# A two-block transformer kernel: 16 latent-attention heads between the steps of a projection, full 128-column tiles, bias rows loaded from a shifted table, negated differential scores

## The chip, the cores and the metric

The program runs on one core of one Trainium2 chip and is launched once. The metric is the device time of an execution in microseconds. The kernel before was timed three times: 2095.17, 2100.26 and 2096.01 us, the median is 2096.01 us.

## The reference

The input is 512 tokens of width 1024, everything in fp32. Two transformer blocks run one after the other. The change concerns only the attention of the first; the second block (sparse attention, a gated delta rule, a mixture of 32 experts) and the first block's FFN are the same in both kernels.

The first block computes `z = rms_norm(x) @ w_in` and splits it into latents for one attention (MLA) and queries, keys and values for another (differential):

```python
# MLA: 8 heads, width 96 (64 + 32 with rope), values 64 wide
q = (rms_norm(q_lat) @ w_uq);  kv = (rms_norm(kv_lat) @ w_ukv)
k = concat([k_nope, broadcast(k_rope)]);  q, k = rms_norm(q), rms_norm(k)   # then rope
logits = where(allowed, q @ k.T * 96 ** -0.5, -1e30)
y_mla = softmax(logits) @ v
# differential: 4 heads, two queries and two keys of width 64 each (m = 0, 1), values 128 wide
logits[m] = where(allowed, rms_norm(dq[m]) @ rms_norm(dk[m]).T * 64 ** -0.5 + bias, -1e30)
probs = softmax(logits)
y_diff = rms_norm((probs[0] - lam * probs[1]) @ dv) * (1 - lam_init)
# both
x = x + concat([y_mla, y_diff]) @ w_out
```

`allowed` lets a query see the keys of its own chunk of 64 tokens and of all chunks before it. `bias` is a table of 32 rows per head, looked up by a bucket of (key position - query position).

## The kernel before

The first block's attention is `block1_attention`. Tokens lie in four blocks of 128; the three projections of `w_in` behind the latents (`grp` 1: differential keys, 2: differential values, 0: differential queries) are sums over 8 slices of 128 channels, each with three matmuls, since every fp32 operand is split into a high and a low part in TensorE's fast fp32 form (L469 to L471). In plain fp32, which scores, transposes and value products use, the trace shows two instructions for each matmul of the program and one for each transpose.

- *Bias* (L416 to L440). A matmul makes the row `fv` of 640 values for each head, one for each difference of positions. The row goes to a buffer `fd` in DRAM, on ScalarE's queue. Four loads (L436) read it with overlapping rows, row p starting at element p; that is the bias mirrored along the queries, so a matmul with a flipped identity (`flip`, L438) turns it over and VectorE copies it out (L439) and masks a corner (L440).
- *MLA heads' inputs.* The generator `heads()` (as `bg`) makes queries, keys and values of the MLA heads; its steps stand between the matmuls of `grp` 1 and 2.
- *Queries' projection.* `grp` 0 is computed last, slice by slice for all four token blocks, then written out, squared and summed; `turn()` normalises and transposes each block, and its steps are spread over the attention (`next(turns, None)`).
- *Steps of the attention.* `mla_step(i, hp)` handles two MLA heads of query block i, with keys 0 to 128(i+1): scores (L526, PSUM pool `acc`), maximum (L528, VectorE), exponential and its sum (L531, ScalarE), reciprocal (L533) and scaling of the probabilities (L534, VectorE); in a second part transposes (L541) and their copy to SBUF (L543); in a third the value product (L552), with V as the stationary operand: two 64-column tiles side by side in the array, so that the output comes out transposed. `diff_step(i, h)` does the same for one differential head with two score tiles: four matmuls of 64 rows by 64 columns (L566), two each at the same time in different quarters of the array, then bias and maximum in one VectorE operation, a negation (L575), exponentials, two reciprocals, and their combination; transposes at L590, value product at L598.
- *Order.* It is written out by hand: `steps` holds 12 MLA steps (blocks 0 to 2), 16 differential steps, 4 MLA steps (block 3). Each round starts a step's first part, then runs the next part of the steps still open (`pend`). The attention's first step follows the queries' projection.
- *Queues and pools.* SP's queue carries the weights, ScalarE's and GpSimd's the small tensors. `self.adp`, the pool of the second block's `w_ada` tiles (loaded by GpSimd's queue at L862), is allocated ahead of the attention, on the other side of SBUF.

## Time and profile before

| | before |
|---|---|
| median of 3 runs | 2096.01 us |
| profiled execution, own time | 2101.31 us |
| its span, first to last instruction | 2099.5 us |
| mean granted TensorE clock | 0.979 |
| TensorE busy | 1995.3 us (95%) |
| VectorE busy | 1206.0 us (57%) |
| ScalarE busy | 734.9 us (35%) |
| GpSimd busy | 218.0 us (10%) |

The profile comes from one execution. Its times count from the first instruction. PE is TensorE, PEld its loading of stationary operands (beside the matmuls), DVE VectorE, ACT ScalarE, POOL GpSimd. A matmul counts as busy from its start to its modelled end, so matmuls overlap in the records and the step from one start to the next says more than a duration. "L552" is a line of the kernel; "O<-PT,V" are the tiles written and read. In brackets stands the idle time ahead of an instruction and what ended it. In the 2099.5 us, the attention that the change touches ends near 242 us.

### The profile page before, as it was taken

Reading aid. Unit: us, or ns where it says so; the run is one execution under the profiler, and the core shown is the slowest. Engines: PE = TensorE matmul, PEld = TensorE weight load, DVE = VectorE, ACT = ScalarE, POOL = GpSimd, SP = SyncE. Lnnn points to the kernel's source line nnn. Section 1 sums busy time; section 2 is a strip of 40 time slices with the busy share of each in tenths; the row PEclk is TensorE's granted clock in tenths of the full one; section 3 lists DMA queues with packets and bytes.
Section 4 is the critical chain, followed back from the end, with each engine's and each line's share of the span. In section 5 each row is a group of like instructions: output and inputs, shape, how many; then the busy total and the mean of one; then the engine's idle time right before and its main releaser. Section 6 shows DMA issues by size and latency. Waiting matters only on the chain.

```text
span 2099.5 us, 33715 instructions
## 1 busy us (share of the span) xinstructions
PE 1995.3 (95%) x12921; PEld 1395.7 (66%) x12921; DVE 1206.0 (57%) x2577; ACT 734.9 (35%) x1405; POOL 218.0 (10%) x227
## 2 busy tenths in 40 slices
PE   8999999999999998998989989999988999999995
PEld 6764788788888777676777878788854444444441
DVE  5867678666666757898384674554465223223234
ACT  4456533232233434335253544542222122122121
POOL 0000001000100013013131131010003000000000
PEclk9998999999999999999999999999989999999998
DMA  7210237554532432122111211263677999999991
GB/s 235 61 41 11 77 123 221 161 170 144 184 101 91 146 112 71 41 86 71 47 51 42 96 36 47 96 221 117 239 294 289 396 389 398 392 387 401 394 388 58
DMA packets 110795, 363.43 MB, mean 173 GB/s; under 512 B 12646, under 2 KB 16766, under 8 KB 110626
## 3 DMA queue, kind: packets, MB, share of 16 engines
q1 hardware_dynamic: 98100, 325.57, 42.9%
q0 software_dynamic: 8528, 30.94, 4.7%
q10 hardware_dynamic: 4002, 4.72, 0.7%
q8 instruction: 104, 1.70, 0.3%
q14 instruction: 61, 0.50, 0.1%
HBM read 349.60 MB, written 11.57 MB: 172 GB/s over the span
## 4 chain that ended last, share of the span: by engine, by line
PE 76%; DVE 13%; DMA 4%; issue 3%; ACT 3%; POOL 0%; ACTq 0%; DVEq 0%; SPq 0%; POOLq 0%
PE acc L1943 15%; PE acc L278 10%; PE acc L275 10%; PE acc L276 10%; PE pb L1309 3%; DVE cv L1197 3%; DMA adw<-in_w_ada 2%; PE acc L1911 1%; PE acc L1912 1%; DVE wlo L253 1%; PE pz L1984 1%; PE pz L1985 1%; PE fl L933 1%; PE fl L942 1%; PE fl L934 1%
## 5 line engine op out<-in xcount | busy, mean ns | idle before, releaser
L252 ACT ACTIVATE whi<-wraw 128x1024 fp32r<-128x1024 f32 (+5 forms) x196 | 191.9, 979 | 316.5 <-PE acc L276 237.5
L253 DVE TENSOR_TENSOR wlo<-wraw,whi 128x1024 fp32r<-128x1024 f32 (+5 forms) x181 | 206.2, 1140 | 95.6 <-PE acc L278 49.4
L1943 PE MATMUL acc<-mraw,XT 128*32 128x512 f32 x1796 | 208.3, 592 | 0.0
L275 PE MATMUL acc<-h_hi,whi 128*128 128x512 f32 x408 | 165.8, 406 | 5.2 <-DVE t L998 3.0
L275 PE MATMUL acc<-x_hi,whi 128*128 128x512 f32 x416 | 166.1, 399 | 0.0
L276 PE MATMUL acc<-x_lo,whi 128*128 128x512 f32 x416 | 164.2, 395 | 0.0
L276 PE MATMUL acc<-h_lo,whi 128*128 128x512 f32 x408 | 162.7, 399 | 0.2 <-DVE h_lo L836 0.2
L1943 PEld LDWEIGHTS acc<-mraw,XT 128*32 128x32 f32 x1796 | 60.5, 110 | 133.1 <-issue 124.7
L1990 DVE TENSOR_TENSOR VT<-VT,pz 128x512 f32<-128x512 f32 x120 | 76.1, 683 | 65.6 <-PE pz L1985 65.6
L1953 DVE TENSOR_TENSOR a<-a,acc 128x512 f32<-128x512 f32 x16 | 11.0, 687 | 172.5 <-PE acc L1943 172.5
L278 PE MATMUL acc<-x_hi,wlo 128*128 128x512 f32 x416 | 106.8, 395 | 0.0
L1943 PE MATMUL acc<-mraw,AT 128*32 128x512 f32 x896 | 103.8, 595 | 0.0
L278 PE MATMUL acc<-h_hi,wlo 128*128 128x512 f32 x408 | 103.7, 394 | 0.0
L275 PEld LDWEIGHTS acc<-h_hi,whi 128*128 128x128 f32 x408 | 77.8, 191 | 23.1 <-DVE t L998 3.4
L275 PEld LDWEIGHTS acc<-x_hi,whi 128*128 128x128 f32 x416 | 78.2, 188 | 19.5 <-issue 0.5
L278 PEld LDWEIGHTS acc<-x_hi,wlo 128*128 128x128 f32 x416 | 78.2, 188 | 18.9
L276 PEld LDWEIGHTS acc<-x_lo,whi 128*128 128x128 f32 x416 | 78.2, 188 | 18.7 <-issue 0.5
L276 PEld LDWEIGHTS acc<-h_lo,whi 128*128 128x128 f32 x408 | 77.8, 191 | 16.4 <-issue 0.6
L278 PEld LDWEIGHTS acc<-h_hi,wlo 128*128 128x128 f32 x408 | 76.3, 188 | 16.8 <-issue 0.7
L1197 DVE SCALAR_TENSOR_TENSOR cv<-G,vecs,cv 128x512 f32<-128x512 f32 x72 | 78.8, 1095 | 11.3 <-ACT cv L1195 10.1
L1975 POOL TENSOR_TENSOR yl<-y,yh 128x512 fp32r<-128x512 f32 x30 | 38.5, 1286 | 406.6 <-ACT yh L1974 402.1
L275 PE MATMUL acc<-a_hi,whi 128*128 128x512 f32 x176 | 70.8, 403 | 5.3 <-ACT a_hi L252 5.2
(620 smaller groups left out, 4089.6 us busy)
## 6 DMA issues: line engine op xcount, KB each, us to landing
mraw<-in_moe_u SPq DMA_DIRECT2D x113, 512.0 KB, 9.9
mraw<-in_moe_g SPq DMA_DIRECT2D x112, 512.0 KB, 7.0
mraw<-in_moe_d SPq DMA_DIRECT2D x112, 512.0 KB, 9.7
wraw<-in_w_in SPq DMA_DIRECT2D x51, 512.0 KB, 3.3
adw<-in_w_ada POOLq DMA_DIRECT2D x48, 512.0 KB, 5.1
wraw<-in_w_gate SPq DMA_DIRECT2D x22, 512.0 KB, 3.8
wraw<-in_w_up SPq DMA_DIRECT2D x22, 512.0 KB, 3.7
wraw<-in_w_out SPq DMA_DIRECT2D x16, 512.0 KB, 3.6
```

The costliest lines, as they stand in the source:

```text
L252: nc.scalar.activation(hi, src, AF.Copy)
L253: (sub or nc.vector).tensor_tensor(lo, src, hi, op=OP.subtract)
L275: mm(ps, lhsT=a, rhs=xh(k), start=first and j == 0, stop=False)
L276: mm(ps, lhsT=a, rhs=xl(k), start=False, stop=False)
L278: mm(ps, lhsT=wl[:, j * P:(j + 1) * P], rhs=xh(k), start=False, stop=last and j == n - 1)
L933: mm(ps, lhsT=a, rhs=self.HH[:, 4 * hf + k, :], start=hf + k == 0, stop=False)
L934: mm(ps, lhsT=a, rhs=self.HL[:, 4 * hf + k, :], start=False, stop=False)
L1197: nc.vector.scalar_tensor_tensor(cv, G[:, j:j + S], w(j), cv, op0=OP.mult, op1=OP.add)
L1309: mm(pp[r, u, :], lhsT=v3(lhsT)[r, u, :], rhs=I64[r] if rhs is None else v3(rhs)[r, u, :], start=True, stop=True)
L1943: mm(ps[n][o:o + size, :], lhsT=XT[:, k, o:o + size], rhs=unit(m, half, s, kk), start=k == 0, stop=k == nk - 1)
L1975: split.tensor_tensor(lo, f, hi, op=OP.subtract)
L1990: nc.vector.tensor_tensor(x, x, pz, op=OP.add)
```

## The change

- *Bias.* The table row is written to DRAM once for each of the 128 partitions ([4, 128, 640]); four loads with a row step of 639 elements then read it already turned. Write, loads and the corner's masks go to GpSimd and its queue. The flip, its matmuls and VectorE's copies and masks go. `fd` is now read from row `P - 1` on.
- *MLA, blocks 0 and 1.* 16 steps of a single head each (`ahead`). `slot()`, called after every second group of three projection matmuls of `grp` 0, starts one such step and advances the open ones. Scores and transposes share the PSUM pool `ptr` (tag `tr`, two buffers); VectorE makes all copies of the transposed probabilities. For `grp` 0 two weight slices are loaded at once and the second half runs token block by token block, each written out (`evict`) when it is complete.
- *MLA, all blocks.* The value product has the transposed probabilities as the stationary operand (128 columns) and 64 columns of V moving. Probabilities are no longer scaled; `mla_out(i)` takes one reciprocal of the 8 heads' sums, scales the output, and transposes it (4 transposes per block).
- *Differential.* Queries lie zero-padded in two 128-row tiles (`dq_tile`: `q[:, t, m]` holds rows 64m to 64m+63, the other half is cleared by GpSimd), so a score is one 128x128 matmul per m. `tensor_tensor_reduce` now multiplies by -1 and takes the minimum, and the exponential has scale -1, so no negation stands between. One reciprocal serves both m.
- *Order.* `steps` becomes mla_out(0), one step of block 2, mla_out(1), the other three of block 2, three differential steps, mla_out(2), 13 differential steps, block 3; mla_out(3) runs inside the output projection. `self.adp` is allocated behind the attention.

The diff, cut to its core:

```diff
         bias = sm([P, DH, S], "bias", 1)
...
-        fd = dp.tile([DH, 640], F32, name="fd")
-        nc.scalar.dma_start(fd[:], fv)
+        fd = dp.tile([DH, P, 640], F32, name="fd")
+        nc.gpsimd.dma_start(fd[:], fv.unsqueeze(1).broadcast_to([DH, P, 640]))
         for h in range(DH):
-            bt = sm([P, S], "P", 4)
-            src = fd[h:h + 1, 0:S]
-            nc.scalar.dma_start(bt, bass.AP(tensor=src.tensor, offset=src.offset, ap=[[1, P], [1, S]]))
-            pb = self.psc.tile([P, S], F32, tag="sc", name=self.nm("pb"))
-            mm(pb, lhsT=flip, rhs=bt, start=True, stop=True)
-            nc.vector.tensor_copy(bias[:, h, :], pb)
-            nc.vector.memset(bias[0:64, h, 448:512], NEG)
+            src = fd[h, 0:1, 0:S]
+            nc.gpsimd.dma_start(bias[:, h, :], bass.AP(tensor=src.tensor, offset=src.offset + P - 1, ap=[[639, P], [1, S]]))
+            nc.gpsimd.memset(bias[0:64, h, 448:512], NEG)
...
+        def mla_pv(i, h, pT):
+            if h == 0:
+                Os[i] = self.psc.tile([P, S], F32, tag="sc", name=self.nm("O"))
+            for kb in range(i + 1):
+                mm(Os[i][:, h * 64:(h + 1) * 64], lhsT=pT[:, kb * P:(kb + 1) * P],
+                   rhs=mla[kb][1][:, h * 64:(h + 1) * 64], start=kb == 0, stop=kb == i)
+        def mla_out(i):
+            nc.vector.reciprocal(sus[i], sus[i])
+            on = sm([P, MLA_H, 64], "qs", 2)
+            nc.vector.tensor_tensor(on, Os[i].rearrange("p (h d) -> p h d", h=MLA_H),
+                                    sus[i].unsqueeze(2).broadcast_to([P, MLA_H, 64]), op=OP.mult)
+            yield
+            pt = self.ptr.tile([P, S], F32, tag="tr", name=self.nm("ptr"))
+            for k in range(4):
+                nc.tensor.transpose(pt[:, k * P:(k + 1) * P], on[:, 2 * k:2 * k + 2, :], self.ident)
...
+        def mla_step(i, heads, pool, tag, sep):
...
+            for h in heads:
+                sc = pool.tile([P, S], F32, tag=tag, name=self.nm("sc"))
+                mm(sc[:, :n], lhsT=mla[i][0][:, h, :], rhs=kT[:, h, :n], start=True, stop=True)
+                mx = sm([P, 1], "mx", 6)
+                nc.vector.tensor_reduce(mx, sc[:, :n], axis=AX.X, op=OP.max, negate=True)
+                pr = sm([P, S], "P", 4)
+                nc.scalar.activation(pr[:, :n], sc[:, :n], AF.Exp, bias=mx, accum_out=sus[i][:, h:h + 1])
...
+                (nc.vector.tensor_copy if j or sep else nc.scalar.copy)(pT[:, :n], pt[:, :n])
...
+        ahead = [mla_step(i, (h,), self.ptr, "tr", True) for i in range(2) for h in range(MLA_H)]
+        live = []
+        def slot():
+            new = [ahead.pop(0)] if ahead else []
+            for g in new:
+                next(g)
+            live[:] = [q for q in live if next(q, 1) is None] + new
...
+        def dq_tile():
+            q = sm([P, NT, 2, DH, P], "wu", 1)
+            nc.gpsimd.memset(q[64:128, :, 0], 0.0)
+            nc.gpsimd.memset(q[0:64, :, 1], 0.0)
+            return q
...
+                if kks == (2, 3):
+                    order = [(k, w, t) for t in range(NT) for k, w in ks]
...
+                    if grp == 0:
+                        if n % 2:
+                            slot()
+                        if k == KD - 1:
+                            evict(grp, t, ps[t], zs, st)
...
-            for half in range(2):
-                for m in range(2):
-                    c = (half + m) % 2
-                    mm(scs[m][64 * c:64 * c + 64, :n],
-                       lhsT=dq_st[64 * m:64 * m + 64, i, h, 64 * c:64 * c + 64],
-                       rhs=dkT[64 * m:64 * m + 64, h, :n], start=True, stop=True)
+            for m in range(2):
+                mm(scs[m][:, :n], lhsT=dq_st[:, i, m, h, :], rhs=dkT[:, h, :n], start=True, stop=True)
...
-                nc.vector.tensor_tensor_reduce(pr[:, :n], scs[m][:, :n], bias[:, h, S - n:], 1.0, -3e38,
-                                               OP.add, OP.max, mx)
-                nmx = sm([P, 1], "nmx", 4)
-                nc.vector.tensor_scalar(nmx, mx, -1.0, None, op0=OP.mult)
...
+                nc.vector.tensor_tensor_reduce(pr[:, :n], scs[m][:, :n], bias[:, h, S - n:], -1.0, 3e38,
+                                               OP.add, OP.min, mx)
...
+                nc.scalar.activation(pr[:, :n], pr[:, :n], AF.Exp, bias=mx, scale=-1.0, accum_out=su[:, m:m + 1])
...
-        mlas = [mla_step(i, hp) for i in range(NT) for hp in range(MLA_H // 2)]
-        steps = mlas[:12] + [diff_step(i, h) for i in range(NT) for h in range(DH)] + mlas[12:]
+        mlas = {i: [mla_step(i, (h, h + 1), self.pacc, "acc", False) for h in range(0, MLA_H, 2)] for i in (2, 3)}
+        diffs = [diff_step(i, h) for i in range(NT) for h in range(DH)]
+        steps = [mla_out(0)] + mlas[2][:1] + [mla_out(1)] + mlas[2][1:] + diffs[:3] + [mla_out(2)] + diffs[3:] + mlas[3]
```

How the instructions move is shown at three places. Numbers in the names are buffer numbers; each row is an instruction of the program.

TensorE at the end of the queries' projection, before: the last projection matmuls (L469 to L471), then the first score matmuls of block 0 (L526), then its first transpose (L541).

```order
L470 MATMUL acc_1102<-wlo_1196,h_hi 128x512
L471 MATMUL acc_1102<-whi_1195,h_lo 128x512
L526 MATMUL acc_1247<-kT_337,qT_464 128x128
L526 MATMUL acc_1257<-kT_337,qT_464 128x128
L526 MATMUL acc_1267<-kT_337,qT_464 128x128
L526 MATMUL acc_1277<-kT_337,qT_464 128x128
L526 MATMUL acc_1295<-kT_337,qT_464 128x128
L526 MATMUL acc_1305<-kT_337,qT_464 128x128
L526 MATMUL acc_1326<-kT_337,qT_464 128x128
L541 MATMUL ptr_1287<-ident,P_1251 128x128
```

The same engine in the second half of that projection, in the changed kernel: projection matmuls are L550 to L552, scores L484, transposes L494, value products L459.

```order
L550 MATMUL acc_1080<-whi_1233,h_hi 128x512
L551 MATMUL acc_1080<-wlo_1234,h_hi 128x512
L552 MATMUL acc_1080<-whi_1233,h_lo 128x512
L484 MATMUL sc_1186<-kT_316,qT_444 128x128
L459 MATMUL O_1140<-V_410,PT_1178 128x64
L494 MATMUL ptr_1193<-ident,P_1173 128x128
L550 MATMUL acc_1080<-whi_1233,h_hi 128x512
L551 MATMUL acc_1080<-wlo_1234,h_hi 128x512
L552 MATMUL acc_1080<-whi_1233,h_lo 128x512
L484 MATMUL sc_1203<-kT_316,qT_444 128x128
```

Scores, a value product and a transpose of three different heads now stand between the groups of three projection matmuls, where they all stood behind the last of them.

GpSimd's order from the start of the program, in the changed kernel: the table's write (L430), the clearing of the query tile (L518, L519; `wu` also held the weights of the MLA keys and values until then), the bias loads and masks (L433, L434), then the second block's `w_ada` (L895, L897), which in the kernel before is the first work of this queue.

```order
L430 DMA fd<-qs_296 512x1x640
L518 MEMSET wu_1083 64x4x512
L519 MEMSET wu_1083 64x4x512
L433 DMA bias_295<-fd 128x512 x4
L434 MEMSET bias_295 64x64 x4
L895 COPY adw_2716<-rsy_2621 128x1
L895 COPY adw_2720<-rsy_2621 128x1
L897 DMA adw_2716<-in_w_ada 128x1024
```

The loads stand behind the two memsets on this engine, and these write a tile that TensorE reads until the last matmul of the MLA keys and values.

TensorE in the differential stretch, before: two heads' scores as 64-row, 64-column tiles (L566), the transposes of a head (L590) and value products (L598).

```order
L566 MATMUL acc_2079<-dkT_347,wu_1223 64x384
L566 MATMUL acc_2080<-dkT_347,wu_1223 64x384
L566 MATMUL acc_2116<-dkT_347,wu_1223 64x384
L566 MATMUL acc_2117<-dkT_347,wu_1223 64x384
L566 MATMUL acc_2116<-dkT_347,wu_1223 64x384
L566 MATMUL acc_2117<-dkT_347,wu_1223 64x384
L598 MATMUL O_1941<-zA_1091,PT_2022 128x128
L598 MATMUL O_1941<-zA_1093,PT_2022 128x128
L590 MATMUL ptr_2073<-ident,P_1997 128x128 x3
L566 MATMUL acc_2159<-dkT_347,wu_1223 64x512
```

And in the changed kernel: scores L600, transposes L621 (of probabilities) and L645 (of a block's output), value products L629.

```order
L600 MATMUL acc_1968<-dkT_326,wu_1083 128x512
L600 MATMUL acc_1969<-dkT_326,wu_1083 128x512
L600 MATMUL acc_1995<-dkT_326,wu_1083 128x512
L600 MATMUL acc_1996<-dkT_326,wu_1083 128x512
L645 MATMUL ptr_1952<-ident,qs_1898 128x128 x4
L621 MATMUL ptr_1962<-ident,P_1911 128x128 x3
L600 MATMUL acc_2043<-dkT_326,wu_1083 128x512
L629 MATMUL O_1924<-zA_1071,PT_1966 128x128
```

A head's scores are two matmuls over all 128 rows and columns where they were four over quarters of the array. SP's order is the same in both kernels, and behind the attention so is that of every engine.

## Rows read from the trace of the kernel before

**Rows 1.** Windows: start:end, length us; busy us of each engine; clock; DMA.
```profile
45.00:108.00 63.00, 62.52 (x282) 45.62 (x281) 52.99 (x176) 28.00 (x43) 0.00 (x0) 1.00 0.21 65
108.00:132.50 24.50, 24.28 (x113) 19.34 (x112) 15.38 (x35) 7.86 (x10) 0.00 (x0) 1.00 0.27 87
132.50:167.30 34.80, 32.17 (x180) 19.47 (x178) 27.14 (x102) 20.88 (x67) 0.00 (x0) 0.90 0.00 1
167.30:211.50 44.20, 41.76 (x244) 20.03 (x242) 34.09 (x174) 30.54 (x91) 0.00 (x0) 0.85 0.04 13
211.50:242.50 31.00, 28.93 (x189) 20.33 (x189) 20.91 (x77) 19.46 (x43) 0.00 (x0) 1.00 0.04 10
```
The busy columns are PE, PEld, DVE, ACT, POOL, with the number of instructions; then granted clock, DMA share, GB/s.

**Rows 2.** Timeline of TensorE, bias: start, length (us), line, operation, tile, shape, count.
```profile
34.59 2.93 PE L438 MATMUL pb<-P,lat 128*128 128x512 f32 x6
...
39.70 0.40 PE L471 MATMUL acc<-whi,h_lo 128*128 128x512 f32 x1
```

**Rows 3.** Timeline of TensorE behind the queries' projection (brackets: idle, releaser).
```profile
132.59 0.83 PE L526 MATMUL acc<-kT,qT 100*128 100x128 f32 x6
133.60 0.49 PE L526 MATMUL acc<-kT,qT 100*128 100x128 f32 x2 [0.17 <-DVE zq L492]
136.06 1.19 PE L526 MATMUL acc<-kT,qT 100*128 100x128 f32 x6 [1.98 <-ACT P L531]
```

**Rows 4.** Timeline of TensorE, value products and transposes (128*64: a 64-column tile).
```profile
153.03 0.43 PE L552 MATMUL O<-PT,V 128*64 128x128 f32 x2
153.39 0.66 PE L508 MATMUL ptr<-ident,zq 128*128 128x128 f32 x4
153.98 0.65 PE L552 MATMUL O<-PT,V 128*64 128x128 f32 x6
154.56 0.33 PE L541 MATMUL ptr<-ident,P 128*128 128x128 f32 x1
```

**Rows 5.** One line's instructions: duration ns min/median/max, first and last start us.
```profile
L1508 PE MATMUL prc<-gw,ones x16: 279/279/300, 1481.3 to 1483.0; 128*128 128x36 f32 x16
```

**Rows 6.** Windows of 5 us; the granted clock stands behind the five engines.
```profile
140.00:145.00 5.00, 5.00 (x21) 2.69 (x20) 2.62 (x11) 2.13 (x10) 0.00 (x0) 0.58 0.00 0
185.00:190.00 5.00, 5.00 (x18) 1.99 (x20) 2.63 (x18) 2.27 (x7) 0.00 (x0) 0.50 0.00 0
```

**Rows 7.** Timeline of TensorE: the last matmul of the MLA keys and values.
```profile
106.81 1.10 PE L676 MATMUL pkv<-wu,lat 128*128 128x512 f32 x2
```

**Rows 8.** DMA issues, 0 to 60 us: queue, count, KB each, median us to landing.
```profile
P<-fd ACTq DMA_DIRECT2D x4, 256.0 KB, 5.3
```

**Rows 9.** Timeline of TensorE: differential scores, and full-width scores of block 3.
```profile
199.88 1.08 PE L566 MATMUL acc<-dkT,wu 64*64 64x512 f32 x6
200.89 0.55 PE L590 MATMUL ptr<-ident,P 128*128 128x128 f32 x3
201.37 1.81 PE L566 MATMUL acc<-dkT,wu 64*64 64x512 f32 x8
203.11 0.94 PE L598 MATMUL O<-zA,PT 128*128 128x128 f32 x6
...
223.61 1.02 PE L526 MATMUL acc<-kT,qT 100*128 100x512 f32 x2
224.47 1.06 PE L598 MATMUL O<-zA,PT 128*128 128x128 f32 x8
```

**Rows 10.** VectorE by line, 131 to 241 us: busy us, mean ns | idle before.
```profile
L534 DVE TENSOR_SCALAR P<-P,ri 128x128 f32<-128x128 f32 (+3 forms) x32 | 11.9, 378 | 0.1
...
L533 DVE RECIPROCAL ri<-su 128x1 f32<-128x1 f32 x32 | 4.9, 157 | 2.5 <-ACT P L531 2.3
...
L557 DVE TENSOR_TENSOR y_lo<-O,y_hi 128x512 fp32r<-128x512 f32 x4 | 2.7, 687 | 0.5 <-ACT y_hi L556 0.5
```

**Rows 11.** Groups by form, 131 to 160 us: a head's exponential and maximum.
```profile
L531 ACT ACTIVATE P<-acc,mx 128x256 f32<-128x256 f32 x8 | 3.7, 470 | 0.6 <-DVE mx L528 0.6
...
L528 DVE TENSOR_REDUCE mx<-acc 128x1 f32<-128x256 f32 x8 | 3.1, 411 | 0.0
```

## The prediction, made blind

> **What bounds the kernel now.** I read the stages first (busy time per window), then TensorE's order of time inside them, then VectorE's groups. The change touches only what runs before 242.5 us of a span of 2099.5: behind that point the order of the instructions is the same on all engines, so a shift there reaches the end as it is. In that region TensorE is the engine to watch: it is busy 62.52 of 63 us and 24.28 of 24.5 us in the projections, and 32.17 of 34.8, 41.76 of 44.2 and 28.93 of 31 us in the three windows of the attention [rows 1]. VectorE has 52.99 of 63 us in the first of these and 27.14, 34.09 and 20.91 us in the attention: a close second, never first. [...]

> First, the bias: eight L438 matmuls stand between 34.59 and 39.70 us in the middle of a projection [rows 2]. Second, the turn from the projection to the attention: six score matmuls start at 132.59, two at 133.60, the next only at 136.06, behind 1.98 us of waiting for ScalarE's exponential [rows 3]. Third, changes of the array's form: two L552 matmuls (64 columns wide) take from 153.03 to 153.39, the four transposes behind them until 153.98 [rows 4]. Full-width matmuls with a full stationary tile follow each other after 0.113 us (15 steps in 1.7 us, with only 36 moving columns) [rows 5], so these six would take 0.68 us full; they took 0.95. Two changes cost 0.27 us, 0.14 each. In the TensorE view from 136 to 242 us I count 95 changes between 64-wide and full-width matmuls. [...]

> **The change part by part.**
> *Bias.* TensorE loses the eight L438, VectorE four copies and four memsets, ScalarE's queue the flip, the table's write and four loads. On TensorE this is 39.70 - 34.59 = 5.1 us, less two projection matmuls that run in between (at most 0.40 each, the duration in the second row [rows 2]): 4.3 to 5.1. It is not all paid back if the heads' chain on VectorE then binds (52.99 of 63 busy, so at worst 0). I take **-4.5**, since TensorE has 0.48 us idle in those 63. What is added runs on GpSimd's queue: the write of the shifted table, four loads, six memsets. The order puts the query tile's memsets ahead of the loads, and these wait for the last L676 at 106.8 us [rows 7], as the tile's place is the weights' until then. Behind them come loads of the size that landed in 5.3 us on ScalarE's queue [rows 8]; even one after the other they take 21 us, to 128, and the memsets ahead of them may take 7 more. The first differential scores stand at 167.3, where I cut the third window [rows 1]. Cover some 30 us, cost 0; with the cover gone each late us would stand in front of all of them, on VectorE. The right-hand pool that moves behind the attention costs 0 too: its first instruction waits for the FFN's norm, as before.

> *The turn.* The first 16 heads (blocks 0 and 1) now go between the projection's last matmuls, so that the projection covers their chain. Lost there: 133.60 - 132.59 less six steps of 0.11, and 136.06 - 133.60 less two: 0.35 + 2.24 = 2.6 us. I take **-2.6** (bounds 0 and -3.3, a third gap of that kind).

> *The clock behind it.* [...] Without the idle turn I see no cause for it: **-2** (bounds 0 and -3.5, if the neighbouring windows hold more of it).

> *Full columns.* (a) 95 changes at 0.14 go: 13.3; some are hidden behind waits, I take -13. (b) The 160 probability-times-value matmuls: now full stationary tile, 64 moving columns. Their price lies between the 0.113 at 36 columns [rows 5] and at most 0.15 (a transposes' step with 128 columns and a change in it [rows 4]); I take 0.113, as the step did not feel the columns. Before, six took 0.58 us with one change [rows 4]: (0.58 - 0.14)/6 = 0.073. So 160 x 0.040 = +6.4. (c) Differential scores: four 64x64 tiles in two passes. Started together a step of 512 keys takes 200.89 - 199.88 = 1.01 us, with the first alone 203.11 - 201.37 = 1.74; the full form is two matmuls of 512 columns, each as L526, 224.47 - 223.61 = 0.86: 1.72 [rows 9]. Nothing to 0.71 us per 512 keys, 10 such in all: 0 to 7, I take half, +3.5. (d) 16 new transposes of the normalised output, 0.113 each: +1.8. Sum **-1.3**, bounds -5 (scores at 0) and +8 (0.15 in (b), +7 in (c)).

> [...]

> *VectorE.* Gone are 32 scalings (11.9 us), 32 reciprocals (4.9) and 32 negations as small as these [rows 10]: over 20 us. New are 12 more copies, four merged scalings, four halves of the queries: 20 operations of at most 0.69 [rows 10], most of them narrower, some 9 us. Net about -12 us on an engine that is second. What this can return is TensorE's waiting in the two later windows, 2.44 + 2.07 us [rows 1]: bounds 0 and -4.5, I take **-2.5**.

> *New waits.* In the interleaved stretch each head's scores and transposes share two PSUM buffers, so the next head's scores wait until ScalarE has read this one's, and the projection queues behind them on TensorE. Chain for a head of 256 keys: reduction 0.41, exponential 0.47 [rows 11], with scores of 0.43 (a half of L526's 0.86 [rows 9]): 1.31 us, and the reading of the sum. TensorE has of its own per head those scores 0.43, four value matmuls 0.45, two transposes 0.23 and three projection matmuls at up to 0.4 (0.7 to 1.2): 1.8 to 2.3. It just covers; I take 0.2 us of hand-overs for each of 16: **+3** (0 to 18, below).

> Sum: -4.5 - 2.6 - 2 - 1.3 - 2.5 + 3 = **-9.9 us**. The profiled execution took 2101.3 us and would take 2091.4; the median of the runs is 5.3 lower, 2096.0, so I predict **2086**. A measurement of this kernel tells some 0.3% (6.3 us) from no change.

> **The rivals.**
> *The clock holds throughout, 2076.* If full-width scores keep the clock up in the differential stretch too, 10 us or so at 0.50 [rows 6] give back 5 more; with no new waits (-3) and VectorE's full 4.5 (-2) the sum is -20. For it: the low clock follows 64-wide work. Against: block 0's scores are short in both kernels, and TensorE waits on VectorE there.

> *The tiles were better than I read, 2095.* If value matmuls did run two at a time (0.057, half of 0.113) and scores always four at a time, (b) is +9.0 and (c) +7.1, 6.2 worse than I took; and if VectorE's relief returns nothing, 2.5 more: -1.2. [...] For it: 199.88 to 200.89. Against: 201.37 to 203.11.

> *The heads' chain holds the projection, 2104.* In the interleaved stretch stand some 19 other operations on ScalarE and VectorE: four weight splits on each, twice as wide as the 0.69 us row [rows 10], and eleven exits and sums of the projection of about 0.69. If every one lands between a head's reduction and its exponential, TensorE waits 8 x 1.37 + 11 x 0.69 = 18.5 us. Then -9.9 + 18.5 = +8.6. It decides from 0.6 us of extra waiting per head (9.9/16). Against: VectorE has 15.38 of 24.5 us busy there now and ScalarE 7.86 [rows 1].

> **How the numbers follow.** Forecast 0.62 (its own range 2079 to 2093, of which 0.08 is a gain under 6.3 us), clock 0.16, tiles 0.13, chain 0.09 (0.02 of it within 6.3 us). Faster by over 0.3%: 0.54 + 0.16 = 0.70; within: 0.08 + 0.13 + 0.02 = 0.23; slower: 0.07. The range reaches from 2074 to 2097: it takes in the tiles' case and most of the clock's, and leaves out the chain's and the far end of the clock's.

> **What would show it.** In the changed profile: no 64-wide matmuls before 242 us; no L438 at 35 us and the value projection of the last token block some 4 us earlier than 106.8; score matmuls between the projection's with waits of about 0.2 us each; no half-speed stretch at the turn; attention done near 232.5 instead of 242.5; the same length behind it. Waits for the exponential or the reduction of a microsecond per head in the interleaved stretch would prove the chain; long idle before the differential scores with a bias load as releaser would break my cover.

## The result: 1.4% slower

The changed kernel takes 2128.2 us (median of 4) against 2098.1 us (median of 4 of the kernel before beside it): ratio 1.0142, 95% interval 1.0112 to 1.0172. I had forecast 2086 us, faster.

The loss lies where I had looked only for the flips' gain. The last matmul of the MLA keys and values stood at 106.81 us before [rows 7]; it now stands at 135.77. From there to the first matmul of the FFN it takes as long as before: 280.95 - 106.81 = 174.1 us before, 309.67 - 135.77 = 173.9 now (timeline of TensorE, the kernel before first):

```profile
280.95 0.39 PE L275 MATMUL acc<-x_hi,whi 128*128 128x512 f32 x1
```
```profile
135.77 1.09 PE L711 MATMUL pkv<-wu,lat 128*128 128x512 f32 x2
...
309.67 0.39 PE L274 MATMUL acc<-x_hi,whi 128*128 128x512 f32 x1
```

The windows of [rows 1] in the changed kernel (columns as there):

```profile
45.00:108.00 63.00, 32.22 (x133) 23.51 (x131) 28.08 (x89) 13.11 (x18) 0.00 (x0) 0.76 0.27 59
108.00:132.50 24.50, 24.50 (x108) 17.25 (x106) 21.56 (x81) 10.84 (x16) 0.00 (x0) 1.00 0.23 71
132.50:167.30 34.80, 34.76 (x187) 27.43 (x186) 25.98 (x65) 16.62 (x40) 6.26 (x10) 1.00 0.23 77
167.30:211.50 44.20, 39.82 (x217) 33.53 (x216) 29.81 (x88) 23.63 (x68) 0.00 (x0) 0.81 0.08 25
```

In the first, TensorE is busy 32.22 of 63 us, where it was 62.52. Its two longest waits from 25 to 130 us (what waited and for whom: us, times, longest):

```profile
PE ptr L731 <- DVE qs L747: 20.8, 1, 20.8
PE acc L550 <- ACT whi L251: 9.5, 1, 9.5
```

Together they are 30.3 us, about the 29.0 by which that matmul comes later. Neither VectorE nor ScalarE is the cause. In the chain that ends last (0 to 130 us; start, us, what) both stand behind weight loads:

```profile
33.01 23.71 DMA wraw<-in_w_inB
56.74 1.06 ACT whi L251
57.83 1.24 DVE wlo L252
59.08 22.90 DMA wraw<-in_w_inB
82.06 1.07 ACT whi L251
83.15 1.23 DVE wlo L252
84.38 0.35 DVE qs L747
```

A load of 512 KB takes 23 us; its split (L251, L252) comes late. VectorE sits idle from 72.1 to 83.15 us for it and runs L747, whose operands were written by 72.1, only behind it. Next the DMA issues, 0 to 130 us (what, queue, count, KB, median us to landing of those whose landing the trace has), before and now:

```profile
wraw<-in_w_inB SPq DMA_DIRECT2D x12, 512.0 KB, 3.7
```
```profile
wraw<-in_w_inB SPq DMA_DIRECT2D x12, 512.0 KB, 14.5
...
fd<-qs POOLq DMA_DIRECT2D x1, 1280.0 KB, 54.8
```

The table's write takes 54.8 us. The second median takes in two loads issued before the write; of the loads issued from 32 to 70 us alone, before and now:

```profile
wraw<-in_w_inB SPq DMA_DIRECT2D x6, 512.0 KB, 4.3
```
```profile
wraw<-in_w_inB SPq DMA_DIRECT2D x4, 512.0 KB, 22.9
```

One by one these four took 23.7, 28.4, 22.9 and 17.0 us. The write's packets in the trace's DMA records (5120 bytes each, 256 of them), with the weights' packets of 4096 bytes, counted by their start:

```
from us          30   36   42   48   54   60   66   72   78   84
table's write    32   30   30   27   29   31   29   29   19    0
weight loads    155  100    0   25   25  110   96   16   48  128
```

The write's packets take 773 ns each (median), at most four at a time, from 30.9 to 82.1 us. Of the 128 packets of a weight load some 95 start within 4 us (34 to 38, then 38 to 42); the rest of these two trickle in from 48 us on at 25 per 6 us, and the first of the two loads lands only at 56.72. About a quarter of each is left behind. The profile counts 16 DMA engines, and four of them, one for each of the write's packets in flight, would be a quarter; but which engine moved a packet the records do not say, so this cause is the author's inference.

### The profile page after: what moved, and what is told of

It is laid out like the page before. It is cut to its first block, busy times and chain, and to the rows that moved or that the text cites. A ratio compares the mean times of both kernels' runs of the same rounds, so it can differ in the third digit from the quotient of the medians.

```text
span 2124.7 us, 33496 instructions
## 1 busy us (share of the span) xinstructions
PE 1988.6 (94%) x12865; PEld 1410.4 (66%) x12865; DVE 1199.2 (56%) x2481; ACT 730.6 (34%) x1393; POOL 224.2 (11%) x238
## 4 chain that ended last, share of the span: by engine, by line
PE 75%; DVE 12%; DMA 7%; issue 3%; ACT 3%; POOL 0%; ACTq 0%; DVEq 0%; SPq 0%; POOLq 0%
PE acc L1978 15%; PE acc L274 11%; PE acc L277 11%; PE acc L275 11%; PE pb L1344 3%; DMA wraw<-in_w_inB 3%; DVE cv L1232 2%; DMA adw<-in_w_ada 2%; PE acc L1946 1%; PE acc L1947 1%; PE pz L2019 1%; PE pz L2020 1%; DVE wlo L252 1%; PE fl L968 1%; PE fl L977 1%
## 5 line engine op out<-in xcount | busy, mean ns | idle before, releaser
L251 ACT ACTIVATE whi<-wraw 128x1024 fp32r<-128x1024 f32 (+5 forms) x196 | 191.9, 979 | 340.2 <-PE acc L275 242.0
L252 DVE TENSOR_TENSOR wlo<-wraw,whi 128x1024 fp32r<-128x1024 f32 (+5 forms) x181 | 205.9, 1138 | 125.1 <-ACT whi L251 75.2
L277 PE MATMUL acc<-x_hi,wlo 128*128 128x512 f32 x416 | 106.8, 395 | 0.0
```

The costliest lines, as they stand in the source:

```text
L251: nc.scalar.activation(hi, src, AF.Copy)
L252: (sub or nc.vector).tensor_tensor(lo, src, hi, op=OP.subtract)
L277: mm(ps, lhsT=wl[:, j * P:(j + 1) * P], rhs=xh(k), start=False, stop=last and j == n - 1)
```

## The experiments

Theory **T**: the table's write holds up the weight loads. Rival **H**, forecast with 0.09: the interleaved heads hold the projection. Ratios are to the kernel before on the same chip, with 95% intervals.

**The bias of before in the changed kernel, and the table alone in the kernel before.** Diffs, the second in the kernel before (and `flip` likewise):

```diff
-        nc.gpsimd.dma_start(fd[:], fv.unsqueeze(1).broadcast_to([DH, P, 640]))
+        nc.scalar.dma_start(fd[:], fv)
...
+            mm(pb, lhsT=flip, rhs=bt, start=True, stop=True)
```
```diff
-        nc.scalar.dma_start(fd[:], fv)
+        nc.gpsimd.dma_start(fd[:], fv.unsqueeze(1).broadcast_to([DH, P, 640]))
```

> The changed kernel with the bias of the kernel before (row of 10 KB, four overlapping loads on ScalarE's queue, flip matmuls, VectorE's copies). Theory T, the table's write: its 256 packets of 5120 bytes run four at a time from 30.9 to 82 us and hold up the weight loads, which moved the last matmul of the MLA keys and values from 106.8 to 135.8 us (+29.0); without it that point is back near 107 and the time is 2128 - 29 = 2099 us (2094 to 2104). Rival H, the heads' chain holds the projection: the loss stays, 2128 us or up to 4.5 more for the flips (2124 to 2135).

> The kernel before with the shifted table alone (write, four loads and masks on GpSimd and its queue; no flips). T: the whole loss appears here, 2098 + 29 = 2127 us (2120 to 2134), with TensorE idle for some 30 us between 45 and 90 us and weight loads of 12 to 24 us there. H: the flips' 4.5 us are gained, 2094 us (2089 to 2098).

Measured: 0.9992 (0.9977 to 1.0008) and 1.0183 (1.0143 to 1.0224). Without the table the loss is gone; the table alone makes it, 38 us, more than the 29 expected (2137.9 us, above the range given). In its trace the last matmul of the MLA keys and values stands at 140.02 us, 33.2 later than before, and the granted clock from there to the FFN is 0.91, where it was 0.94. H falls.

**A write of 10 KB, and a copy that is spread.** The diff is the second's; the first writes the row `fv` to `fd` once.

```diff
-        nc.gpsimd.dma_start(fd[:], fv.unsqueeze(1).broadcast_to([DH, P, 640]))
+        nc.gpsimd.dma_start(fs[:], fv)
+        nc.gpsimd.dma_start(fd[:], fs[:].unsqueeze(0).broadcast_to([P, DH, 640]))
```

> The changed kernel with the row of 10 KB written once instead of 1.28 MB, and the four loads with a row step of +1: it leaves out the turning of the bias along the queries, so it prices a write that costs nothing. T: 2128 - 33.5 = 2095 us (2088 to 2099), the 29.0 and the forecast 4.5. H: 2128 us. Under T what is left against before is the rest of the change: my forecast for it was -5.4, the trace after shows some -0.2 from 106.8 (135.8) us on.

> The changed kernel with the table made in two steps on GpSimd's queue: the row of 10 KB to DRAM, then a copy from DRAM to DRAM with the 128 rows as the outer dimension; the loads take a row step of 2559. The same 1.28 MB are written. T in the form 'four rows on four partitions, so four packets at a time': the copy spreads over all engines, is done in some 5 to 13 us and costs at most one late weight load: 2095 to 2101 us. Rival B, the bytes themselves cost: 1.28 MB are still written and now also read, so most of the loss stays, 2118 us or more. H: 2128 us.

Measured: 0.9951 (0.9934 to 0.9967) and 0.9940 (0.9919 to 0.9962), that is 10 and 13 us under the kernel before. The copy writes the same bytes and costs nothing that can be measured against the small write (1.5 us less, within the noise; it came out below the range given), so B falls: it is not the bytes. How many engines moved the table the records do not say, here and with the rows in all partitions below. In its trace:

```profile
wraw<-in_w_inB SPq DMA_DIRECT2D x12, 512.0 KB, 5.1
...
fd<-fs POOLq DMA_DIRECT2D x1, 1280.0 KB, 9.0
```
```profile
101.11 1.09 PE L713 MATMUL pkv<-wu,lat 128*128 128x512 f32 x2
...
268.62 0.39 PE L274 MATMUL acc<-x_hi,whi 128*128 128x512 f32 x1
```

**A quarter of the table.** `fd` of 32 rows a head, 16 loads of 32 rows.

> The changed kernel with the table written for 32 rows instead of 128, still from four partitions, and 16 loads of 32 rows in place of 4. Theory T (four packets at a time, and a load waits only while the write lasts): the write ends after some 13 us, near 44 us, before the load that TensorE wants at 48 us has to be there, so the loss is gone but for 0 to 4 us: 0.994 to 0.996 of before. Rival S, the loss goes with the bytes: a quarter of the 42 us between the changed kernel and the spread copy stays, 10 us, 0.999 of before.

Measured: 0.9971 (0.9957 to 0.9984), 6 us above the spread copy and between T and S. The write lands after 15.4 us and the MLA matmul stands at 106.62 us, 5.5 later than with the spread copy; TensorE waits 4.3 us for L749. So even a write of some 12 us is not wholly covered, against what I had thought; the loss does not go strictly with the bytes either (a quarter of them costs 5.5 of 34.7 us there).

**Another queue, another buffer.**

```diff
-        nc.gpsimd.dma_start(fd[:], fv.unsqueeze(1).broadcast_to([DH, P, 640]))
+        nc.scalar.dma_start(fd[:], fv.unsqueeze(1).broadcast_to([DH, P, 640]))
```
```diff
-        fv = sm([DH, 640], "qs")
+        fv = sm([DH, 640], "fv", 1)
```

> The changed kernel with the table's write on ScalarE's queue instead of GpSimd's; its four loads stay on GpSimd's. Theory T (four source partitions, four packets at a time, whatever the queue): the loss up to the last matmul of the MLA keys and values stays, that matmul near 135 us, 1.010 to 1.015 of before. Rival D (GpSimd's queue is the slow thing): the write lands in under 15 us and the time is that of the spread copy, 0.994. The order of the attention in this kernel is nearly that of the spread copy, so the stage behind 135 us should take 193 to 195 us under 'the order costs the other 6 us' and 199 to 200 if the slow write itself does.

> The changed kernel with a tile of its own for the table's row, so that no tile of the MLA queries has to wait until the write has read it. T (the weight loads wait): no difference, 1.012 to 1.017 of before, TensorE idle for some 30 us between 48 and 85 us as in the changed kernel. Rival R (the held buffer stops VectorE and with it everything): the loss goes, 0.994 to 0.998.

Measured: 1.0105 (1.0080 to 1.0130) and 1.0127 (1.0097 to 1.0157). Neither GpSimd's queue nor the held buffer is the cause; T stands. With the write on ScalarE's queue the stage behind, to the first matmul of the FFN, takes 173.1 us (133.28 to 306.42); the expectation counts to a matmul 25.8 us later, so that is 199 in its terms and speaks against the order as what costs the other 6. But with a quick write the stage takes 167.5 (spread copy) or 171.6 and 171.9 us (two runs below), so it varies too much to settle that.

**Why the write is slow.** The same bytes from 128 partitions (after a load that spreads the row); the four rows on partitions 32 apart; each row in 32 partitions, made by the matmul itself:

```diff
+        nc.gpsimd.dma_start(stg, fs[:].unsqueeze(0).broadcast_to([P, DH, 640]))
+        nc.gpsimd.dma_start(fd[:], stg)
```
```diff
+        nc.vector.tensor_copy(rw, rb.unsqueeze(2).broadcast_to([32, DH, 32]))
...
-            mm(pf, lhsT=rb, rhs=t5[:, a:b], start=True, stop=True)
+            mm(pf, lhsT=rw, rhs=t5[:, a:b], start=True, stop=True)
...
+        nc.gpsimd.dma_start(fd[:], fv[0:P:32].unsqueeze(1).broadcast_to([DH, P, 640]))
```
```diff
+        nc.gpsimd.dma_start(fd[:].rearrange("h (q r) j -> (h q) r j", q=32), fv.unsqueeze(1).broadcast_to([P, 4, 640]))
```

> The changed kernel with the row of 10 KB written to DRAM, loaded into all 128 partitions of a tile, and the table written from these 128 partitions: still from SBUF, the same 1.28 MB written, more bytes read. T (the four source partitions are the limit): the write lands in some 5 to 10 us and the time is within 3 us of the spread copy, 0.992 to 0.996 of before. Rival W (a write of this size from SBUF is slow, and the copy was fast because it went from DRAM to DRAM): 1.005 or more.

> The changed kernel with the table's four rows on partitions 0, 32, 64 and 96 instead of 0 to 3 (the matmul that makes them writes all 128 partitions; the write reads four of them). In the changed kernel the 256 packets of 5120 bytes ran four at a time, 773 ns each, while the first without a neighbour took 196 to 202 ns. Theory F (four DMA engines, each as slow as that by itself): packets of some 773 ns again, the write takes 51 us, 1.010 to 1.017 of before. Theory G (neighbouring partitions share one way out of SBUF and the four packets take turns on it): with the rows apart the packets take half or a quarter of that, 200 to 400 ns, the write some 13 to 27 us, and the last matmul of the MLA keys and values stands between 106 and 121 us: 0.997 to 1.005 of before. [...]

> The changed kernel with the same matmul writing each head's row to 32 partitions, and the table written from all 128, four rows from each: one write, no second copy. T: 16 engines take part, the write lands in some 4 to 8 us, no weight load waits; within 3 us of the spread copy, 0.992 to 0.996 of before. Rival W2 (only DRAM as source, or the second hop's later start, made the spread copy cheap): 1.000 or more.

Measured: 0.9951 (0.9932 to 0.9970), 1.0017 (1.0001 to 1.0032) and 0.9943 (0.9921 to 0.9965). The write of the last two (rows apart, rows in all):

```profile
fd<-qs POOLq DMA_DIRECT2D x1, 1280.0 KB, 30.8
```
```profile
fd<-qs POOLq DMA_DIRECT2D x1, 1280.0 KB, 7.5
```

The packets took 393 ns (median) with the rows 32 partitions apart and 196 ns with them in all 128. In the changed kernel the last packet, with no neighbour left, took 196; the expectation's "first without a neighbour" is a misreading, as the packets of 198 to 202 ns in the write's first 2 us had others beside them. Why these were quick is open. Same bytes, same packets, and four at a time in both slow versions: 773 is near four times 196 and 393 twice, which would fit four of them taking turns on one way out of SBUF, and two on each of two. F falls, and with the first and the last version W and W2; G stands, though by these times alone: no record shows which way a packet took. The last version is also the simplest repair: one write, no second hop.

**The rest of the change**, each on the spread copy (2089.7 us, on another chip; the kernel before takes 2103.2 us there and 2102.4 here): tiles for the differential scores; blocks 0 and 1 behind the projection; the negation back.

```diff
-                mm(scs[m][:, :n], lhsT=dq_st[:, i, m, h, :], rhs=dkT[:, h, :n], start=True, stop=True)
+                    mm(scs[m][64 * c:64 * c + 64, :n],
+                       lhsT=dq_st[64 * m:64 * m + 64, i, h, 64 * c:64 * c + 64],
```
```diff
-        ahead = [mla_step(i, (h,), self.ptr, "tr", True) for i in range(2) for h in range(MLA_H)]
+        ahead = []
```
```diff
+                nc.vector.tensor_scalar(nmx, mx, -1.0, None, op0=OP.mult)
```

> The changed kernel with the spread copy (that run: 0.9940 of before, 12.6 us under it), but differential queries and scores as before: four 64x64 tiles per head and block, no zero halves. My step (c) with its share of (a): full columns cost 3.5 and save some 28 changes of 0.14, 3.9, so the tiles make no difference, -3 to +4 us. Rival P, tiles do twice the work at a time: full scores cost 7, so the tiles are 3 us or more faster. Rival K, 64-wide work brings the lower clock back: 5 to 10 us slower, with a stretch at half speed between 150 and 200 us in the records.

> The changed kernel with the spread copy, but blocks 0 and 1 of the MLA heads run in pairs behind the queries' projection, as blocks 2 and 3 do. My terms: the turn's 2.6 us and the 2 us of clock come back; the 3 us of new waits are not in the trace of the spread copy (TensorE is busy 37.97 of 38 us from 102 to 140), so +4.6 us (+2 to +8). Rival H, the interleaved heads hold the projection: 0 or faster. Rival K2, the clock falls at the turn for longer: +8 or more, with a half-speed stretch right behind the projection.

> The changed kernel with the spread copy, with the maximum and a negation of its own in each differential score again (32 small VectorE operations more, in the chain from score to exponential). My term for VectorE: TensorE has some waits for it in 165 to 190 us, so +1 us (0 to +3). Rival V, VectorE binds the differential stretch (28.35 busy of 35 us in 175 to 210): 32 x 0.17 = 5 us or more.

Measured: 0.9991 (0.9977 to 1.0006), 0.9967 (0.9950 to 0.9985) and 0.9947 (0.9928 to 0.9966), or 2099.1, 2094.6 and 2090.7 us: 9.4, 4.9 and 1.0 over the spread copy. The last is within the noise, and the second hardly out of it, as the intervals overlap (0.9919 to 0.9962 for the spread copy). The tiles' windows (clock behind the five engines), then the spread copy's:

```profile
162.00:192.00 30.00, 27.67 (x158) 13.11 (x158) 21.45 (x96) 20.77 (x68) 0.00 (x0) 0.83 0.00 1
192.00:222.00 30.00, 26.27 (x120) 15.94 (x118) 18.54 (x58) 18.25 (x42) 0.00 (x0) 0.83 0.00 1
```
```profile
162.00:192.00 30.00, 27.10 (x130) 16.87 (x129) 26.23 (x111) 24.15 (x75) 0.00 (x0) 1.00 0.00 1
192.00:222.00 30.00, 25.70 (x156) 18.28 (x154) 20.19 (x60) 18.14 (x42) 0.00 (x0) 1.00 0.00 1
```

0.83 in 30 us, twice, is some 10 us lost (2 x 0.17 x 30), as much as the 9.4. But these are two executions 18.6 us apart: the tiles' was slower than their median, the spread copy's the fastest of its ten. Over all runs the mean granted clock is 0.9793 with tiles (12 runs) and 0.9824 with the spread copy (10); 0.0031 of 2100 us is an estimated 6.5 us at most, and the mean times are 9.6 us apart. Some 3 us are open. P falls; K stands for the larger part. That 64-wide work is what lowers the clock is not shown as such: with the rows in all partitions, which has full columns, 192 to 222 us stands at 0.83 too, and 162 to 192 at 1.00.

## Why the prediction was wrong

**The step that failed** is the bias. I wrote "What is added runs on GpSimd's queue: the write of the shifted table, four loads, six memsets", and then priced the loads (21 us) and memsets (7), asked only whether they come in time, and closed with "Cover some 30 us, cost 0". The write, 1280 KB, has no price there at all. The row I used for the loads, 256 KB in 5.3 us [rows 8], would have given it 26 us, and 4.3 us for a weight load stood in the same view. The question that I asked came out as forecast: the four bias loads were issued from 140.5 us on, the last mask was set at 148.0, and the first VectorE operation that reads them starts at 203.6. Above all I asked whether the result is late, not what the transfer takes from others: in that stretch the kernel before issues a weight load about every 7 us. In place of cost 0 the runs show 34.7 us up to the MLA matmul (135.77 against 101.11 with the spread copy), and in all 42 us between the changed kernel and the spread copy (1.0142 - 0.9940 of 2098). Most of what is left of the 42 lies between that matmul and the FFN, 173.9 against 167.5 us, with a granted clock of 0.95 against 1.00.

**The rest of the sum** came out near its total, and that was partly luck: with the write repaired the kernel is 12.6 us (spread copy) and 12.0 us (rows in all) faster than before, where I had -9.9. Much of that is clock. The runs' mean granted clock is 0.9784 before (25 runs) and 0.9824 with the spread copy (10); 0.004 of 2100 us is an estimated 8 us at most, where I had -2. The profiles agree: from the MLA matmul to the FFN the kernel before has 0.94 in 174.1 us, some 10 us lost, the spread copy 1.00 in 167.5. And the changed kernel with the bias of before, which is the rest of the change without the flips' gain, is only 1.7 us faster than before (4.8 faster to 1.7 slower), where my other terms sum to -5.4. By its terms:

- *Flips, -4.5.* Right. That kernel and the spread copy differ in the bias alone: the last matmul of the queries' projection stands at 144.07 and 139.81 us, 4.3 apart. (From 106.81 to 101.11 us it would be 5.7, but that includes what else moved ahead of the MLA matmul.)
- *Turn -2.6, clock behind it -2, new waits +3.* Undoing the interleaving costs 4.9 us, close to 2.6 + 2, but not by these terms. With the heads behind the projection TensorE waits 1.6 us at the turn again:

```profile
131.62 0.49 PE L486 MATMUL sc<-kT,qT 100*128 100x128 f32 x2 [1.00 <-DVE zq L528]
132.69 0.33 PE L496 MATMUL ptr<-ident,P 128*128 128x128 f32 x1 [0.58 <-ACT P L490]
```

No run shows the -2 for the clock: 140 to 145 us had 0.58 before [rows 6], but with the heads behind the projection again the clock does not fall, 1.00 from 102 to 192 us. What the other 3 us are is open. The new waits were not there: in the changed kernel a head's step, between projection matmuls, shows no idle time:

```profile
158.21 0.39 PE L484 MATMUL sc<-kT,qT 100*128 100x128 f32 x2
158.44 0.33 PE L459 MATMUL O<-V,PT 128*128 128x64 f32 x2
158.61 0.28 PE L494 MATMUL ptr<-ident,P 128*128 128x128 f32 x1
158.64 0.48 PE L550 MATMUL acc<-whi,h_hi 128*128 128x512 f32 x1
158.96 0.39 PE L551 MATMUL acc<-wlo,h_hi 128*128 128x512 f32 x1
159.19 0.40 PE L552 MATMUL acc<-whi,h_lo 128*128 128x512 f32 x1
159.43 0.38 PE L484 MATMUL sc<-kT,qT 100*128 100x128 f32 x2
```

- *Full columns, -1.3.* Mis-sized for the scores: full ones are 9.4 us better than tiles, not even with them, and the larger part of that is clock, which I had left out of this term and kept for the rival "the clock holds" (0.16). In the one profile of the spread copy there is no half-speed stretch in the attention at all (1.00 from 102 to 242 us). I had also misread a row: the 1.01 us at 199.88 [rows 9] hold six matmuls, where a step has eight, as the row at 201.37 does; two more stand ahead of a value product:

```profile
198.01 1.07 PE L566 MATMUL acc<-dkT,wu 64*64 64x512 f32 x2 [0.16 <-DVE mx L572]
199.01 0.94 PE L598 MATMUL O<-zA,PT 128*128 128x128 f32 x6
```

So no row shows a step done in 1.01 us; the whole one, 1.74, is as long as the full form's 1.72, and (c) was nearer 0 than +3.5. The value products and the changes of form were not tried by themselves.
- *VectorE, -2.5.* Of it the negation is 1.0 us, not told from nothing; the rest of the term was not tried by itself.

From the MLA matmul to the FFN the versions with full columns and a cheap write take 167.5 (spread copy) to 171.9 us (from 128 partitions) against 174.1 before: -2 to -7, where I had -5.4. Their granted clock there is 1.00 (spread copy) to 0.97 (rows in all), against 0.94 before, which can account for all of it: that the turn, the columns and VectorE shortened this stage apart from the clock is not shown. In the changed kernel this stage gained nothing (173.9): it has a clock of 0.81 from 167.3 to 211.5 us. The version with a buffer of its own stands at 173.9 there too, and the one with the write on ScalarE's queue at 173.1. Why the clock falls there in these three was not tried.

## What to carry to other kernels

A transfer that replaces compute can have a price even if nothing waits for its result: ask how many source partitions it reads, how long its packets take, and which loads run beside it. Here the broadcast written from four neighbouring partitions was the bad case, 54.8 us to landing; with the rows put into all 128 partitions by the matmul it was 7.5, and 9.0 with a first hop through DRAM. When a wait names a compute engine, follow the chain back: here ScalarE and VectorE only passed on a late load. And before a gain is booked to the terms of a forecast, compare the granted clock of the runs: a sum can come out right by it.

## What the runs showed of the hardware

```profile
147.76 0.78 PE L461 MATMUL O<-V,PT 128*128 128x64 f32 x6
148.38 0.61 PE L473 MATMUL ptr<-ident,qs 128*128 128x128 f32 x4
```
